# The entry of the in-projection: a written order for VectorE and ScalarE until the second row is there

## The chip, the cores and the metric

The kernel runs on one core of one Trainium2 chip. The metric is the device time of one execution in microseconds (us). The engines are called as the profile calls them: PE (TensorE, matrix products; PEld are its weight loads), DVE (VectorE), ACT (ScalarE), POOL (GpSimd) and SP (SyncE, which issues the transfers from memory here).

## The reference

The reference is one inference step of a two-layer diffusion backbone. Two groups of 128 tokens, a prompt and a sample, go through the same weights; the model width D is 2048. Layer 0 mixes latent attention and grouped-query attention behind one combined in-projection, layer 1 uses differential attention; each layer ends in a gated convolutional feed-forward part. What the change touches is the very beginning of layer 0:

```python
mod = jax.nn.silu(cond) @ w_ada[l] + b_ada[l]
sh1, sc1, gt1, sh2, sc2, gt2 = jnp.split(mod[:, None, :], 6, axis=-1)
h = rmsnorm(x, g_norm_mix[l]) * (1 + sc1) + sh1
...
proj = h @ w_in
```

So the shift `sh1` and the scale `sc1` come out of a product of the condition with two of the six column blocks of `w_ada`; the tokens are normalised, scaled and shifted; and the result `h` is multiplied by `w_in`, a matrix of 2048 rows and 2880 columns. Everything is in float32.

## The kernel before

**Tiling.** Features lie on the 128 partitions, and the 2 x 128 tokens side by side in the free dimension (`NT` = 256). `h` is therefore cut into 16 rows of 128 features, "row k" below, and `w_in` into blocks of 128 x 128: 16 rows by `NIN` = 23 output columns. Every product is made of three matmuls, since a value is held as a high part (rounded to the type that PE multiplies fast) and a low part (the rest): high weight by high row, high weight by low row, low weight by high row. Three such matmuls with one block are called a chain link here, or a chain for short where only one row is at hand.

**Weights.** `Stream` (from L303 on) brings `w_in` in raw tiles of 16 blocks (1 MB; three buffers) with `fetch` on SP. `block` hands out one block after the other; when it has none left it cuts a piece from the raw tile, 4 blocks the first time and 8 later, and `split` (L225) makes the two parts: a cast on ACT (`wh`, L226) and a subtraction on DVE (`wl`, L227). There are four buffers for `wh` and four for `wl`.

**Modulation by units.** `Early` computes shift and scale for one row (the first four units) or for two rows (the other six). `load(1)` and `load(0)` bring the two pieces of `w_ada` (tiles `araw` and `condb`) on SP; `sums` (L412) multiplies them with the condition, with 32 small matmuls for a unit of one row; `turn` (L420) copies the result from the accumulator to `am` on ACT; `finish` transposes `am` on PE (L427) and makes `mod` and `scl` from it by three small instructions on DVE (L430, L433, L435).

**Norm.** The squares of `x` are added up by ACT and DVE, PE takes the mean (L846), `rstd` finishes it with one instruction on DVE (L189) and a power on POOL (L193), `diagonal` writes it on two diagonals (DVE, L213) and `spread` (PE, L221) spreads it over all partitions; that is `rb0`.

**A row.** `modulate` makes row `c`: `x` by `rb0` on DVE (L587), scale and shift for the one half of the tokens on DVE (L595) and for the other on ACT (L598), the high part `hx` by a cast on ACT (L599), the low part by a subtraction (L582) on DVE for even rows and POOL for odd ones.

**Order of the work.** PE runs an order that is written out: each of its instructions in this stage is pinned behind the one before it by `keep_in_program_order`. The order begins with unit 0's first sums, the mean of the norm, unit 0's second sums, the spread, unit 0's transposes and unit 1's first sums. Then `held` runs row 0 through columns 0 to 9 (`HELD` = 10; their accumulators stay in five banks) with unit 1's second sums after column 1 and its transposes after column 4, then row 1 through the same ten columns, and `others` runs rows 0 and 1 through columns 10 to 22 with the sums of units 2 and 3 between them. Then come rows 2 and 3, and from there four rows at a time. The transfers of this stage that are shown as `pin` are pinned on SP in the same manner. On DVE and ACT nothing is pinned in the entry: a planner that steps through the program with its own estimate of every duration and landing puts an instruction where its engine is free and its inputs are taken to be there. So the cast of a later piece of weights can come ahead of a step that the next row waits for. An engine runs its instructions in the planned order and does not pass one that waits.

Of the kernel before, what the change touches and what calls it, by code (L numbers as in the profile page):

```python
# [22 lines left out]
NT = 2 * T  # L23
# [5 lines left out]
EPS = 1e-6  # L29
# [59 lines left out]
def step_kernel(ctx: ExitStack, tc: tile.TileContext, A: dict):  # L89
    nc = tc.nc  # L90
    pe, dve, act, pool, sp = nc.tensor, nc.vector, nc.scalar, nc.gpsimd, nc.sync

    keep = ctx.enter_context(tc.tile_pool(name="keep", bufs=1))
    wpool = ctx.enter_context(tc.tile_pool(name="wpool", bufs=3))
    tmp = ctx.enter_context(tc.tile_pool(name="tmp", bufs=2))
# [37 lines left out]
    x = T_(keep, [P, KD, NT], "x")  # L133

    mod = T_(keep, [P, NL, 6, KD, 2], "mod")
    scl = T_(keep, [P, NL, 2, KD, 2], "scl")
# [9 lines left out]
        tc.keep_in_program_order(sp.dma_start(out=ada["cw"], in_=A["wconv"][:, l]))  # L146


    chains = []

    def step():
# [31 lines left out]
    def rstd(cols, n, factor=1.0, out=None):  # L183

        v = T_(small, [P, 2], "rv")
        at = 0
        for ps in cols:
            w = n // len(cols)
            dve.tensor_scalar(out=v[:, at:at + w], in0=ps, scalar1=EPS, scalar2=factor ** -2,  # L189
                              op0=ALU.add, op1=ALU.mult)  # L190
# [19 lines left out]
    def diagonal(r, cols):  # L210
        dg = T_(tmp, [P, 2 * T], "diag", bufs=1)
        for i, c in enumerate(cols):
            dve.tensor_scalar(out=dg[:, i * T:(i + 1) * T], in0=ident, scalar1=r[:, c:c + 1],  # L213
                              scalar2=None, op0=ALU.mult)
        return dg

    def spread(dg, cols=(0, 1), bank=bank):

        ps = bank()
        n = len(cols) * T  # L220
        pe.matmul(ps[:, :n], ones, dg[:, :n], start=True, stop=True)  # L221
        return ps[:, :n]


    def split(out_hi, out_lo, src, pin=lambda i: i):  # L225
        pin(act.copy(out_hi, src))  # L226
        pin(dve.tensor_tensor(out=out_lo, in0=src, in1=out_hi.bitcast(F32), op=ALU.subtract))  # L227
# [72 lines left out]
    class Stream:  # L300
# [7 lines left out]
        def fetch(self, pin=lambda i: i):  # L308
# [3 lines left out]
            self.raws.append((raw, self.sizes[self.at]))  # L312
            self.at += 1

        def block(self):
            if not self.blocks:
                if not self.raws:
                    self.fetch()
                raw, n = self.raws[0]
                m = min(8, n - self.lo) if self.lo or self.at > 2 else 4  # L320
                wh = T_(wpool, [P, 1024 + P], "wh", F32R, bufs=4)[:, :m * P]
                wl = T_(wpool, [P, 1024 + P], "wl", F32R, bufs=4)[:, :m * P]
                split(wh, wl, raw[:, self.lo * P:(self.lo + m) * P])
                self.blocks = [(wh[:, b * P:(b + 1) * P], wl[:, b * P:(b + 1) * P]) for b in range(m)]
                self.lo += m
                if self.lo == n:
                    self.raws.pop(0)
                    self.lo = 0
            return self.blocks.pop(0)

    def by_token(pieces, xs, outs, first, last):
# [58 lines left out]
    class Early:  # L390
# [26 lines left out]
        def turn(self):  # L417
            n = 2 * self.n
            am = T_(tmp, [P, 512], "am", bufs=1)
            act.copy(am[:, :n * P], self.ps[:, :n * P])  # L420
            self.am = am

        def finish(self):
            n = 2 * self.n
            pt = att_bank()
            for b in range(n):
                tc.keep_in_program_order(pe.transpose(pt[:, b * P:(b + 1) * P], self.am[:, b * P:(b + 1) * P], ident))  # L427
            c = slice(self.c0, self.c0 + self.n)
            out = mod[:, 0, 0:2, c]
            dve.tensor_reduce(out=out, axis=AX.X, op=ALU.add,  # L430
                              in_=pt[:, :n * P].rearrange("p (j c g r) -> p j c r g", j=2, g=4, r=32)[:, :, :, 0:2])
            bada = C("bada").rearrange("p (l j k) -> p l j k", l=NL, j=6)
            dve.tensor_tensor(out=out, in0=out, op=ALU.add,  # L433
                              in1=bada[:, 0, 0:2, c, None].to_broadcast([P, 2, self.n, 2]))
            dve.scalar_tensor_tensor(out=scl[:, 0, 0, c], in0=mod[:, 0, 1, c], scalar=1.0, op0=ALU.add, op1=ALU.mult,  # L435
                                     in1=C("gmix")[:, c, None].to_broadcast([P, self.n, 2]))

    def vector(name, l, j, q):

# [277 lines left out]
    def mixer_ab(hx, W, units, st):  # L717
        l = 0
        with tc.tile_pool(name="ab", bufs=1) as ab:
            with tc.tile_pool(name="abp", bufs=1) as pj:  # L720
# [118 lines left out]
                for to, of in ((squares[0], squares[1]), (squares[0], squares[2]), (squares[0], squares[3]),  # L839
                               (pr[:, 0:2], pr[:, 2:4])):  # L840
                    dve.tensor_tensor(out=to, in0=to, in1=of, op=ALU.add)
                units[0].sums(1)
                ps = bank()
                for g in range(2):
                    for k in range(2):
                        tc.keep_in_program_order(pe.matmul(ps[:, g:g + 1], pr[:, k, g * T:(g + 1) * T], inv(D),  # L846
                                                           start=(k == 0), stop=(k == 1)))
                units[0].sums(0)
                r = rstd([ps[:, 0:2]], 2)
                units[0].turn()  # L850
                units[0].finish()
                rb0 = spread(diagonal(r, (0, 1)))

                def product(ps, c, ks, first, last):
                    pin = (lambda i: i) if free[0] else tc.keep_in_program_order
# [58 lines left out]
                held(banks_, [0], rows, at(c1=[lambda: u1.sums(0), u1.turn, lambda: W.fetch(pin), lambda: load(u3), lambda: W.fetch(pin)],  # L914
                                           c4=[lambda: end(u1)]))
                held(banks_, [1], rows, at())
                others(rows, at(c10=[lambda: u2.sums(1)], c12=[lambda: u2.sums(0), u2.turn], c14=[lambda: end(u2)],
                                c17=[lambda: u3.sums(1)], c20=[lambda: u3.sums(0), u3.turn], c22=[lambda: end(u3)]))
                for q in range(4):
                    banks_ = side()  # L920
                    if q == 0:
                        rows = range(2, 4)
                        held(banks_, [2], rows, at())
                        held(banks_, [3], rows, at())
                    else:
                        u = units[2 * q + 3]
                        rows = range(4 * q, 4 * q + 4)
# [17 lines left out]
            with tc.tile_pool(name="abh", bufs=1) as hp:  # L945
# [36 lines left out]
                for h in range(0, 8, 2):  # L982
                    for i in range(2):
                        ps = gemm(WQ.chunk(), qh, qlo)
# [3 lines left out]
                    ps = gemm(WQ.chunk(), qh, qlo)  # L988
# [7 lines left out]
                    for i in range(2):  # L996
# [3 lines left out]
                        ps = gemm(WK.chunk(), kh, klo, 3 * T)  # L1000
# [219 lines left out]
    with banks("pab") as ppool["ada"]:  # L1220
# [3 lines left out]
        units = [Early(k, 1) for k in range(4)] + [Early(c, 2) for c in range(4, KD, 2)]  # L1224
        W = Stream(A["w_in_ab"], ([TB] * 5 + [12]) * 4)
# [13 lines left out]
    with tc.tile_pool(name="cc", bufs=1) as cp, banks("pc") as ppool["ada"]:  # L1239
        ada["junk"] = lambda: T_(cp, [P, 4, 512], "junk", BF16, bufs=1)  # L1240
        ppool["att"] = ppool["ada"]
        W = Weights(A["w_in_c"], KD, 1)
        hx, ready, todo = modulated(st, 1, 0, W, True)
# [4 lines left out]
        W = Weights(A["w_up"][1], KD, 1)  # L1248
        hx, ready, todo = modulated(st, 1, 1, W, True)
# [153 lines left out]
```

## Time and profile before

| | |
|---|---|
| median of the runs | 2328.17 us |
| lowest and highest of 3 runs | 2324.3 and 2330.32 us |
| the profiled execution | 2326.47 us |
| its span, from the first to the last instruction | 2324.7 us |
| PE busy in the span | 2278.1 us |
| bytes moved | 610.82 MB, 263 GB/s on average |

The rows shown below come from several views. The page counts busy time for each engine. The waits say which engine stood still for whom. A row of the timeline begins with the start and the busy time of an instruction (or of several like ones, "x32"), then engine, line, operation, output <- inputs; a bracket at its end gives the idle time ahead of it and what ended it. A row of the windows gives a stretch, its length, the busy time of PE, PEld, DVE, ACT and POOL with their counts, the granted clock of PE, the share of the DMA engines and the rate of transfer.

### The profile page before, as it was taken

How to read it: one execution, taken by the hardware profiler on the slowest of the kernel's cores; microseconds unless marked ns; L12 is line 12 of the kernel's file. 1: busy time of each engine (PE TensorE's matmuls, PEld its weight loads, DVE VectorE, ACT ScalarE, POOL GpSimd, SP SyncE). 2: the span in 40 equal slices, each digit the busy share in tenths (PEclk: the TensorE clock that was granted, in tenths of full speed). 3: DMA queues.
4: the chain of work that ended last, by engine and by line, in shares of the span. 5: the costliest groups of instructions: out<-in, count | busy, mean ns of one | idle time of the engine just before them, and what ended most of it. 6: DMA issues, size and time to landing. Idle time of an engine off the chain costs nothing. (4 is left out here: it accounts for less than half of the span.)

```text
span 2324.7 us, 47404 instructions
## 1 busy us (share of the span) xinstructions
PE 2278.1 (98%) x19810; PEld 2186.6 (94%) x19810; DVE 1827.7 (79%) x2654; ACT 1178.2 (51%) x1866; POOL 145.6 (6%) x133
## 2 busy tenths in 40 slices
PE   6999999999999999999999999999999999999998
PEld 6888878799999999999989999898999999999998
DVE  4667749789989999999869989787899755666654
ACT  4347554555554355554465555446555434555553
POOL 0002001200000000002210000022000000000011
PEclk9999999999999999999999999999999999999999
DMA  9997789666777777777767787785677555555553
GB/s 388 364 376 254 280 315 386 258 250 252 272 259 285 289 279 257 263 266 278 272 237 274 276 316 297 296 312 222 236 256 272 186 196 200 190 192 200 191 192 125
DMA packets 92566, 610.82 MB, mean 263 GB/s; under 512 B 9984, under 2 KB 17856, under 8 KB 20544
## 3 DMA queue, kind: packets, MB, share of 16 engines
q1 hardware_dynamic: 92352, 607.80, 70.8%
q8 instruction: 155, 2.54, 0.4%
q14 instruction: 59, 0.48, 0.1%
HBM read 603.01 MB, written 4.75 MB: 261 GB/s over the span
## 5 line engine op out<-in xcount | busy, mean ns | idle before, releaser
L226 ACT CAST wh<-raw 128x1024 fp32r<-128x1024 f32 (+1 forms) x789 | 793.7, 1012 | 927.7 <-PE acc L375 694.4
L227 DVE TENSOR_TENSOR wl<-raw,wh 128x1024 fp32r<-128x1024 f32 (+1 forms) x789 | 924.6, 1187 | 315.5 <-ACT wh L226 305.6
L374 PE MATMUL acc<-hx,wh 128*128 128x256 f32 x3440 | 952.6, 277 | 1.3 <-ACT wh L226 0.8
L375 PE MATMUL acc<-hx,wh 128*128 128x256 f32 x3440 | 951.8, 277 | 0.0
L378 PE MATMUL acc<-hx,wl 128*128 128x256 f32 x3440 | 951.6, 277 | 0.1
L374 PEld LDWEIGHTS acc<-hx,wh 128*128 128x128 f32 x3440 | 646.0, 188 | 7.7 <-issue 5.0
L378 PEld LDWEIGHTS acc<-hx,wl 128*128 128x128 f32 x3440 | 645.7, 188 | 5.4 <-issue 3.4
L375 PEld LDWEIGHTS acc<-hx,wh 128*128 128x128 f32 x3440 | 646.1, 188 | 2.7 <-issue 2.5
L484 DVE CUSTOM_DVE_ANT_0 junk<-araw,condb 128x2048 f32<-128x2048 f32 (+1 forms) x192 | 442.8, 2307 | 0.1
L375 PE MATMUL acc<-g,wh 128*128 128x256 f32 x1408 | 388.3, 276 | 0.0
L378 PE MATMUL acc<-g,wl 128*128 128x256 f32 x1408 | 388.0, 276 | 0.0
L374 PE MATMUL acc<-g,wh 128*128 128x256 f32 x1408 | 387.8, 276 | 0.0
L375 PEld LDWEIGHTS acc<-g,wh 128*128 128x128 f32 x1408 | 264.3, 188 | 0.0
L378 PEld LDWEIGHTS acc<-g,wl 128*128 128x128 f32 x1408 | 264.2, 188 | 0.0
L374 PEld LDWEIGHTS acc<-g,wh 128*128 128x128 f32 x1408 | 264.1, 188 | 0.0
L181 POOL TENSOR_TENSOR sqacc<-sqacc,sq 128x256 f32<-128x256 f32 x62 | 85.4, 1377 | 1574.4 <-issue 1298.3
L859 PE MATMUL acc<-hx,wh 128*128 128x256 f32 x608 | 113.7, 287 | 3.9 <-ACT hx L599 3.0
L859 PEld LDWEIGHTS acc<-hx,wh 128*128 128x128 f32 x608 | 93.9, 191 | 12.0 <-issue 4.8
L1172 ACT ACTIVATE cv<-acc,convw 128x256 f32<-128x256 f32 x176 | 98.3, 559 | 2.4 <-PE acc L362 2.4
L648 DVE SCALAR_TENSOR_TENSOR x<-acc,mod,x 128x128 f32<-128x128 f32 x192 | 58.0, 343 | 41.5 <-PE acc L378 40.5
L1178 DVE SCALAR_TENSOR_TENSOR cv<-acc,convw,cv 128x254 f32<-128x254 f32 x176 | 84.3, 479 | 3.7
L1175 DVE SCALAR_TENSOR_TENSOR cv<-acc,convw,cv 128x254 f32<-128x254 f32 x176 | 83.6, 475 | 2.5 <-ACT cv L1172 2.5
(253 smaller groups left out, 2492.4 us busy)
## 6 DMA issues: line engine op xcount, KB each, us to landing
raw<-w_up SPq DMA_DIRECT2D x176, 1024.0 KB, 4.8
araw<-w_ada SPq DMA_DIRECT2D x160, 1024.0 KB, 5.4
raw<-w_down SPq DMA_DIRECT2D x88, 1024.0 KB, 4.8
raw<-w_in_c SPq DMA_DIRECT2D x48, 1024.0 KB, 5.5
raw<-w_in_ab SPq DMA_DIRECT2D x20, 1024.0 KB, 8.4
araw<-w_first SPq DMA_DIRECT2D x16, 1024.0 KB, 8.7
condb<-w_first SPq DMA_DIRECT2D x16, 1024.0 KB, 10.4
raw<-w_out_ab SPq DMA_DIRECT2D x16, 1024.0 KB, 7.4
```

The source lines that it names most:

```text
L181: pool.tensor_tensor(out=st["acc"], in0=st["acc"], in1=sq, op=ALU.add)
L226: pin(act.copy(out_hi, src))
L227: pin(dve.tensor_tensor(out=out_lo, in0=src, in1=out_hi.bitcast(F32), op=ALU.subtract))
L374: fixed(pe.matmul(ps[:, :n], wh, xh(k), start=(i == 0), stop=False))
L375: fixed(pe.matmul(ps[:, :n], wh, xl(k), start=False, stop=False))
L378: fixed(pe.matmul(ps[:, :n], wl, xh(k), start=False, stop=(i == last)))
L484: tc.keep_in_program_order(dve.tensor_tensor_reduce(out=junk, in0=raw, in1=condb[:, c].rearrange("p (g n) -> p g n", g=4), scale=1.0, scal ...
L648: dve.scalar_tensor_tensor(out=x[:, c, s], in0=ps[:, s], scalar=mod[:, l, 3 * which + 2, c, g:g + 1], in1=x[:, c, s], op0=ALU.mult, op1=AL ...
L859: pin(pe.matmul(ps, w, hx[:, k, lo:lo + NT], start=first and k == ks[0] and n == 0, stop=last and k == ks[-1] and n == 2, skip_group_check ...
L1172: pin(act.activation(y, ps, AF.Identity, scale=cw[:, 1, m:m + 1], bias=cw[:, 3, m:m + 1]))
L1175: pin(dve.scalar_tensor_tensor(out=y3[:, :, 1:], in0=p3[:, :, :T - 1], scalar=cw[:, 0, m:m + 1], in1=y3[:, :, 1:], op0=ALU.mult, op1=ALU.add))
L1178: pin(dve.scalar_tensor_tensor(out=y3[:, :, :T - 1], in0=p3[:, :, 1:], scalar=cw[:, 2, m:m + 1], in1=y3[:, :, :T - 1], op0=ALU.mult, op1=A ...
```

## The change

A new helper `tie` pins an instruction behind the one before it on its engine as long as a flag is set. The flag goes up ahead of `rstd` and down when the second row is there. In between, the instructions of `rstd`, `diagonal`, `spread`, `turn` and `finish` are tied, and so are those of two new functions, `start_row` (the multiply by `rb0`) and `finish_row` (scale, shift, high part, low part), which take the place of `modulate` for rows 0 and 1. The low part of row 1 is thereby made on DVE; it was on POOL.

`Stream.piece(m, pin)` cuts a piece of up to `m` blocks when it is called, and is called at written places: 4 blocks ahead of the spread, 8 behind row 0, 4 when unit 1's second sums are issued, 4 behind row 1. Outside of these places `block` cuts pieces of 8 as before, always of 8 where more than 8 are left of a raw tile.

On PE, unit 1's second sums go from behind column 1 to behind column 3 of row 0, and its transposes from behind column 4 to behind column 6. The two fetches and the loads of unit 3, which are issued on SP, move with the sums.

```diff
+    tied = [False]
+
+    def tie(i):
+        return tc.keep_in_program_order(i) if tied[0] else i
...
@@ class Stream
+        def piece(self, m, pin=lambda i: i):
+            if not self.raws:
+                self.fetch()
+            raw, n = self.raws[0]
+            m = min(m, n - self.lo)
+            wh = T_(wpool, [P, 1024 + P], "wh", F32R, bufs=4)[:, :m * P]
+            wl = T_(wpool, [P, 1024 + P], "wl", F32R, bufs=4)[:, :m * P]
+            split(wh, wl, raw[:, self.lo * P:(self.lo + m) * P], pin)
+            self.blocks += [(wh[:, b * P:(b + 1) * P], wl[:, b * P:(b + 1) * P]) for b in range(m)]
...
         def block(self):
             if not self.blocks:
...
-                m = min(8, n - self.lo) if self.lo or self.at > 2 else 4
...
+                self.piece(8)
             return self.blocks.pop(0)
...
@@ mixer_ab
+                def start_row(c):
+                    h = T_(tmp, [P, NT], "nt", bufs=4)
+                    tie(dve.tensor_tensor(out=h, in0=x[:, c], in1=rb0, op=ALU.mult))
+
+                    def finish_row():
+                        a_, b_ = (lambda g: scl[:, 0, 0, c, g:g + 1]), (lambda g: mod[:, 0, 0, c, g:g + 1])
+                        tie(dve.tensor_scalar(out=h[:, :T], in0=h[:, :T], scalar1=a_(0), scalar2=b_(0),
+                                              op0=ALU.mult, op1=ALU.add))
+                        tie(act.activation(h[:, T:], h[:, T:], AF.Identity, scale=a_(1), bias=b_(1)))
+                        tie(act.copy(hx[:, c, :NT], h))
+                        tie(dve.tensor_tensor(out=hx[:, c, NT:2 * NT], in0=h, in1=hx[:, c, :NT].bitcast(F32),
+                                              op=ALU.subtract))
+
+                    return finish_row
+
                 units[0].sums(1)
...
                 units[0].sums(0)
+                tied[0] = True
                 r = rstd([ps[:, 0:2]], 2)
+                dg = diagonal(r, (0, 1))
+                W.piece(4, tie)
+                rb0 = spread(dg)
                 units[0].turn()
+                first_row = start_row(0)
                 units[0].finish()
-                rb0 = spread(diagonal(r, (0, 1)))
+                first_row()
+                W.piece(8, tie)
...
                 u1, u2, u3 = units[1:4]
-                scale(units[0])
                 load(u2)
                 u1.sums(1)
                 rows = range(0, 2)
                 banks_ = side()
-                held(banks_, [0], rows, at(c1=[lambda: u1.sums(0), u1.turn, lambda: W.fetch(pin), lambda: load(u3), lambda: W.fetch(pin)],
-                                           c4=[lambda: end(u1)]))
+                second = []
+
+                def fresh():
+                    W.piece(4, tie)
+                    second.append(start_row(1))
+                    u1.turn()
+
+                def second_row():
+                    u1.finish()
+                    second[0]()
+                    W.piece(4, tie)
+                    tied[0] = False
+
+                held(banks_, [0], rows, at(c3=[lambda: u1.sums(0), fresh, lambda: W.fetch(pin), lambda: load(u3),
+                                               lambda: W.fetch(pin)],
+                                           c6=[second_row]))
                 held(banks_, [1], rows, at())
```

More of the change, by code (lines that the diff above doesn't have):

```diff
@@ L188, in rstd @@
             w = n // len(cols)
-            dve.tensor_scalar(out=v[:, at:at + w], in0=ps, scalar1=EPS, scalar2=factor ** -2,
-                              op0=ALU.add, op1=ALU.mult)
+            tie(dve.tensor_scalar(out=v[:, at:at + w], in0=ps, scalar1=EPS, scalar2=factor ** -2,
+                                  op0=ALU.add, op1=ALU.mult))
             at += w
@@ L212, in diagonal @@
         for i, c in enumerate(cols):
-            dve.tensor_scalar(out=dg[:, i * T:(i + 1) * T], in0=ident, scalar1=r[:, c:c + 1],
-                              scalar2=None, op0=ALU.mult)
+            tie(dve.tensor_scalar(out=dg[:, i * T:(i + 1) * T], in0=ident, scalar1=r[:, c:c + 1],
+                                  scalar2=None, op0=ALU.mult))
         return dg
@@ L220, in spread @@
         n = len(cols) * T
-        pe.matmul(ps[:, :n], ones, dg[:, :n], start=True, stop=True)
+        tie(pe.matmul(ps[:, :n], ones, dg[:, :n], start=True, stop=True))
         return ps[:, :n]
@@ L313, in fetch @@
             self.at += 1
+        def piece(self, m, pin=lambda i: i):
[7 more added lines that the diff above has]
+            self.blocks += [(wh[:, b * P:(b + 1) * P], wl[:, b * P:(b + 1) * P]) for b in range(m)]
+            self.lo += m
+            if self.lo == n:
+                self.raws.pop(0)
+                self.lo = 0
         def block(self):
             if not self.blocks:
-                if not self.raws:
-                    self.fetch()
-                raw, n = self.raws[0]
-                m = min(8, n - self.lo) if self.lo or self.at > 2 else 4
[L321 to L328, printed above, removed]
+                self.piece(8)
             return self.blocks.pop(0)
@@ L419, in turn @@
             am = T_(tmp, [P, 512], "am", bufs=1)
-            act.copy(am[:, :n * P], self.ps[:, :n * P])
+            tie(act.copy(am[:, :n * P], self.ps[:, :n * P]))
             self.am = am
@@ L429, in finish @@
             out = mod[:, 0, 0:2, c]
-            dve.tensor_reduce(out=out, axis=AX.X, op=ALU.add,
-                              in_=pt[:, :n * P].rearrange("p (j c g r) -> p j c r g", j=2, g=4, r=32)[:, :, :, 0:2])
+            tie(dve.tensor_reduce(out=out, axis=AX.X, op=ALU.add,
+                                  in_=pt[:, :n * P].rearrange("p (j c g r) -> p j c r g",
+                                                              j=2, g=4, r=32)[:, :, :, 0:2]))
             bada = C("bada").rearrange("p (l j k) -> p l j k", l=NL, j=6)
[L433 to L436, printed above, removed]
+            tie(dve.tensor_tensor(out=out, in0=out, op=ALU.add,
+                                  in1=bada[:, 0, 0:2, c, None].to_broadcast([P, 2, self.n, 2])))
+            tie(dve.scalar_tensor_tensor(out=scl[:, 0, 0, c], in0=mod[:, 0, 1, c], scalar=1.0,
+                                         op0=ALU.add, op1=ALU.mult,
+                                         in1=C("gmix")[:, c, None].to_broadcast([P, self.n, 2])))
     def vector(name, l, j, q):
```

## The prediction

> **What bounds the kernel now.** I read the page first, then the waits of PE in the first 40 us, then the clock and the transfers by windows, then the timeline of the two places where PE stands still.
>
> ```profile
> span 2324.7 us, 47404 instructions
> PE 2278.1 (98%) x19810; PEld 2186.6 (94%) x19810; DVE 1827.7 (79%) x2654; ACT 1178.2 (51%) x1866; POOL 145.6 (6%) x133
> ```
>
> PE is busy for 98% of the span, so a microsecond that it loses anywhere arrives at the end, and all of its idle time is 2324.7 − 2278.1 = 46.6 us. Its waits from 0 to 24 us, and from 24 to 40 us (total us, times, longest):
>
> ```profile
> PE ada L412 <- DMA araw<-w_first: 12.8, 1, 12.8
> PE acc L859 <- ACT hx L599: 1.4, 1, 1.4
> ...
> PE acc L859 <- ACT hx L599: 1.6, 1, 1.6
> PE acc L859 <- POOL hx L582: 0.4, 1, 0.4
> ```
>
> The first wait, for the first weights to land, is not touched by the change. The other three are: 1.4 us before the product of row 0, 1.6 us before that of row 1, and 0.4 us for the low half of row 1. Each has a second price, the clock. These windows follow the steps in which the granted clock changes (stretch, its length, busy time of PE, PEld, DVE, ACT and POOL with counts, granted clock, DMA share, GB/s):
>
> ```profile
> 19.58:22.99 3.41, 1.50 (x36) 1.06 (x35) 2.69 (x8) 1.37 (x4) 0.00 (x0) 1.00 1.00 418
> 22.99:26.40 3.41, 3.41 (x38) 2.77 (x38) 0.36 (x1) 0.00 (x0) 0.00 (x0) 0.50 1.02 416
> ...
> 29.82:33.23 3.41, 1.38 (x9) 0.98 (x9) 1.37 (x4) 0.90 (x2) 0.73 (x1) 1.00 1.02 423
> 33.23:36.64 3.41, 3.41 (x18) 3.41 (x17) 0.00 (x0) 1.56 (x3) 0.00 (x0) 0.50 1.01 420
> ...
> 1166.45:1169.86 3.41, 2.23 (x16) 1.20 (x16) 1.80 (x5) 0.74 (x3) 0.70 (x1) 1.00 0.80 195
> 1169.86:1173.27 3.41, 3.41 (x14) 1.13 (x12) 2.80 (x7) 2.19 (x5) 0.62 (x1) 0.50 0.97 396
> 1183.51:1186.93 3.42, 2.38 (x18) 1.97 (x18) 2.95 (x5) 3.40 (x7) 0.88 (x2) 1.00 0.16 22
> 1186.93:1190.34 3.41, 3.41 (x32) 3.41 (x31) 3.29 (x5) 1.78 (x4) 2.67 (x3) 1.00 0.97 392
> ```
>
> A window of 3.41 us with PE busy for 1.50, 1.38 or 2.23 us (44, 40 and 65%) is followed by one at clock 0.50; one with 2.38 us (70%) is not. So each stall in the entry costs half of 3.41 us, 1.7 us, on top of itself.
>
> **Row 0.** PE's fixed order here is the second sums of unit 0, the spread of the norm, unit 0's transposes, unit 1's first sums, the product.
>
> ```profile
> 16.50 1.93 PE L412 MATMUL ada<-condb,condw 128*32 128x128 f32 x32
> ...
> 17.70 2.08 ACT L226 CAST wh<-raw 128x512 fp32r<-128x512 f32 x3 [6.40 <-DMA raw<-w_in_ab]
> ...
> 18.36 1.22 PE L221 MATMUL misc<-diag,cst 128*128 128x256 f32 x2
> ...
> 19.69 0.36 ACT L420 COPY am<-ada 128x256 f32<-128x256 f32 x1
> 20.10 0.44 PE L427 MATMUL att<-cst,am 128*128 128x128 f32 x2 [0.52 <-ACT am L420]
> ...
> 20.47 1.08 PE L412 MATMUL ada<-araw,condw 128*32 128x128 f32 x32
> ...
> 21.37 0.17 DVE L430 TENSOR_REDUCE mod<-att 128x4 f32<-128x16 f32 x1
> ...
> 22.95 1.04 PE L859 MATMUL acc<-hx,wh 128*128 128x256 f32 x2 [1.40 <-ACT hx L599]
> 23.40 0.29 PEld L859 LDWEIGHTS acc<-hx,wh 128*128 128x128 f32 x1 [0.18 <-DVE hx L582]
> ```
>
> The sums end at 16.50 + 1.93 = 18.43, but ACT casts three pieces of weights (4, 8 and 4 blocks) from 17.70 and copies `am` only at 19.69. Tied, it casts one piece of 4 (about a quarter of 2.08 and some start, 0.6) and copies at about 18.5. The transposes then wait only for the spread, to 18.36 + 1.22 = 19.58, and end 0.44 later at 20.02. DVE has the multiply of row 0 behind it and reduces at about 20.07 in place of 21.37: **1.30 us** sooner. From the reduction to the product nothing changes (22.95 − 21.37 = 1.58), so the product starts at 21.65. Unit 1's first sums, 1.08 us, still fit between. In the window to 22.99 PE would be busy for 0.44 + 1.08 + 1.1 = 2.6 us, 77%, above the 70% that kept the clock.
>
> **Row 1.** The same kinds of step, now in the order that the planner chose:
>
> ```profile
> 24.77 1.85 PE L412 MATMUL ada<-condb,condw 128*32 128x128 f32 x32
> ...
> 26.72 1.05 ACT L226 CAST wh<-raw 128x1024 fp32r<-128x1024 f32 x1 [3.82 <-DMA raw<-w_in_ab]
> ...
> 27.68 0.36 ACT L420 COPY am<-ada 128x256 f32<-128x256 f32 x1
> ...
> 28.09 0.44 PE L427 MATMUL att<-cst,am 128*128 128x128 f32 x2 [0.23 <-ACT am L420]
> ...
> 28.73 0.39 PE L859 MATMUL att<-hx,wh 128*128 128x256 f32 x2
> ...
> 28.94 0.17 DVE L430 TENSOR_REDUCE mod<-att 128x4 f32<-128x16 f32 x1
> ...
> 29.41 0.39 PE L859 MATMUL att<-hx,wh 128*128 128x256 f32 x2
> ...
> 30.43 0.41 DVE L587 TENSOR_TENSOR nt<-x,misc 128x256 f32<-128x256 f32 x1
> ...
> 31.86 0.38 PE L859 MATMUL acc<-hx,wh 128*128 128x256 f32 x1 [1.61 <-ACT hx L599]
> ...
> 32.67 0.38 PE L859 MATMUL acc<-hx,wh 128*128 128x256 f32 x1 [0.42 <-POOL hx L582]
> ```
>
> A cast stands ahead of `am`, and subtractions and the multiply of row 1 (30.43) stand between the reduction (28.94) and the product (31.86): 2.92 us, where row 0 took 1.58. A chain of three matmuls is (29.41 − 28.73) / 2 = 0.34 us at full clock. By the new order, step by step: chain 0 starts at 21.65 and waits for its low half as now (23.40 − 22.95 = 0.45), so four chains end at 21.65 + 0.45 + 0.23 + 3 × 0.34 = 23.35. Unit 1's second sums, at the 1.08 of the row at 20.47 and no longer at 1.85, end at 24.43. ACT copies `am` to 24.85 while PE does chains 4 to 6, to 25.5. Transposes to 25.95, reduction at 26.0, plus 1.58: **row 1 starts at 27.58 in place of 31.86, 4.28 us sooner** (the 1.30 included). Chains 7 to 9 fill PE to 27.0, so about 0.6 us of stall stay. The low half moves from POOL to DVE: 32.67 − 31.86 = 0.81 becomes row 0's 0.45, **0.36 us**. With 0.6 + 0.35 us idle in a window PE is busy for 72%, just over the 70% row: the window at half clock goes, **1.7 us**, with the bounds 0 and 1.7 since the margin is thin. Entry together: 4.28 + 0.36 + 1.7 = **6.3 us** (4.6 without the clock).
>
> Edits that I cost at nothing: the next raw tile is cut 4 + 8 + 4 in place of 8 + 8, and the casts above price that: 2.08 for 4 + 8 + 4 against twice 1.05. The piece of 4 and its subtraction, tied ahead of the second `am` and the multiply of row 1, end near 24.6, while PE is in chains 4 to 6; with that cover gone they would cost the 0.6 of a cast. SP's order stays: the third fetch, unit 3's loads and the fourth fetch move with the second sums, which end earlier than now. Behind the tied `am` copy ACT holds row 1's activation and cast, which need it anyway.
>
> **What is late next: the transfers.** The memory queue is full from the start:
>
> ```profile
> 40.00:48.00 8.00, 8.00 (x114) 7.34 (x114) 2.75 (x8) 5.17 (x12) 0.00 (x0) 1.00 1.01 416
> 48.00:54.00 6.00, 6.00 (x76) 5.67 (x75) 4.36 (x11) 4.44 (x10) 0.00 (x0) 1.00 0.89 300
> ...
> 58.00:64.00 6.00, 5.94 (x65) 5.10 (x67) 5.60 (x11) 1.68 (x2) 0.00 (x0) 1.00 0.79 283
> 64.00:78.00 14.00, 13.80 (x164) 10.33 (x160) 10.04 (x21) 5.19 (x8) 0.75 (x1) 1.00 1.00 404
> ```
>
> ```profile
> 67.99 1.19 SPq L403 DMA_DIRECT2D condb<-w_first  x2
> ...
> condb<-w_first SPq DMA_DIRECT2D x2, 1024.0 KB, 7.4
> ...
> 77.56 1.07 PE L412 MATMUL ada<-condb,condw 128*32 128x256 f32 x16 [0.20 <-DMA condb<-w_first]
> ```
>
> It moves some 420 GB/s up to 48 us and has room only in 48 to 54 (300) and 58 to 64 (283): (120 + 137) × 6 / 420 = 3.7 us of transfer; by the DMA shares, (0.11 + 0.21) × 6 = 1.9 us. At 77.56 PE already waits 0.2 us for unit 5's last tile, with no room before it. If PE asks 6.3 us sooner, the idle stretches fill up, and this tile can land 3.7 us sooner and no more (bounds 1.9 and 4.2, the latter with the 404 GB/s of 64 to 78, 16 × 14 / 420 = 0.5 us more). **So 6.3 − 3.7 = 2.6 us come back as one wait at that place.** A stall of 2.6 us lies in one or two windows and should halve the next one (1.7 us); if the first gain is only 4.6, the stall is 0.9 us and does not. I take half of 1.7, 0.85.
>
> The Trainium skill's page "TensorE: Matmul & The Clock Gate", section "HAM oscillation — how this bites in real kernels", gives as rule that PE gaps under about 3.4 us do not bring the clock down. This trace disagrees, since 1.4 and 1.6 us did; by the rule the 0.85 above would be 0.
>
> **Sum.** −6.3 + 2.6 + 0.85 = −2.85 us. Against the profiled execution, 2326.47 us (span 2324.7 and 1.8 around it), that is 2323.6. The median of the runs shown is 2328.17, 1.7 above it, so on that scale 2328.17 − 2.85 = **2325.3 us**. From this cause alone: −1.9 + 1.7 = −0.2 to −6.3, and with the 3 us by which the shown runs stand off their median, 2320.5 to 2330.
>
> **Rivals.** (1) *The transfers do not cap it.* Requests shift in order, other tiles give way, and the whole 6.3 us stays: 2321.9. For it: PE waits only 0.2 us on a transfer after the start. Against it: that wait is at a tile behind a queue with 1.00 share. (2) *The stall at 77.56 does not bring the clock down*, since stalls under a full window do not, in which case the two half-clock windows of the entry have another cause and stay: 3.7 us are left, 2324.5. That is the rule of "TensorE: Matmul & The Clock Gate" in the Trainium skill; for it, one window at 70% kept its clock; against it, three at 65% and less did not. (3) *The order is not as tight as written.* Only listed steps are tied; the next 8-block cast of the second raw tile is not. The planner now puts such a cast ahead of `am`, where it waits for a landing at 26.72. Then `am` comes at 27.7 as before, the reduction at 28.7 (transposes behind it), the product 1.58 later at 30.3: 31.86 − 30.3 + 0.36 = 1.9 us gained, the half clock stays, the transfers do not bind: 2326.3. (4) *Slower: the clock's grid.* Everything after the entry moves by some microseconds against the 3.41 us windows, and gaps that today fall astride two windows fall into one. A place is 1183.51, at 70%, a hair above the 65% that halves. Each such window costs 1.7 us; from two on the 2.85 us are gone, and three make 2328.17 − 2.85 + 5.1 = 2330.4. Against it, the same shift can free windows that are halved today, like the one after 1166.45.
>
> **How the numbers follow.** Forecast 0.40, rival 1 0.17, rival 2 0.14, rival 3 0.14, rival 4 0.15. The range 2320 to 2331 leaves out the lower third of rival 1 (0.06), the upper third of rival 4 (0.05) and the tails of the rest (0.09). About what a measurement of this kernel can tell from no change is 0.3%, 7 us: faster means under 2321.2, slower over 2335.2. Under 2321.2 lie 0.4 of rival 1 (0.07) and the low ends of the others (0.05): 0.12. Over 2335.2 lies only a grid that goes wrong four times and more, 0.05. The rest, 0.83, is within.
>
> **What would show it.** Right: row 0's product near 21.65 and row 1's near 27.6, the cast of 8 blocks behind row 0's hx on ACT, DVE in place of POOL for row 1's low half, no window at 0.50 between 23 and 37 us; then PE waiting 1 to 3 us for `condb` in the sums of unit 5, near 72 to 74 us, and the 48 to 64 us stretches at over 400 GB/s. Wrong: no wait for a transfer there while later stages begin 5 us or more sooner (rival 1); a cast waiting for raw ahead of the second `am` (rival 3); a stall of over 1.2 us in a window without a halved one behind it (rival 2); an entry that gains as written while the end does not, with more windows at 0.50 than now (rival 4).

## The result and the profile after

The changed kernel takes 2323.46 us (median of 20 runs, 2319.56 to 2328.19) where the kernel before, timed beside it, takes 2329.74 us (20 runs, 2323.62 to 2333.61). The ratio is **0.9977, with the interval 0.9969 to 0.9984**: 5.4 us faster, between 3.7 and 7.2. The forecast was 2.85 us faster and 2325.3 us. The profiled execution has a span of 2319.3 us.

The waits of PE in the first 24 us, from 24 to 40 and from 40 to 82 us, in the profile after:

```profile
PE ada L420 <- DMA araw<-w_first: 13.3, 2, 13.0
...
PE acc L890 <- ACT hx L861: 0.6, 1, 0.6
PE acc L890 <- ACT proj L896: 0.2, 1, 0.2
...
PE ada L420 <- DMA condb<-w_first: 1.3, 1, 1.3
PE acc L890 <- POOL hx L592: 0.4, 1, 0.4
PE ada L420 <- DMA araw<-w_first: 0.4, 1, 0.4
```

The 1.4 us ahead of row 0 are gone, of the 1.6 us ahead of row 1 0.6 are left. The wait of 0.4 us for an `araw` tile is new, and the one for unit 5's last `condb` tile has grown from 0.2 to 1.3 us. The timeline after, at the two rows:

```profile
17.90 0.62 ACT L231 CAST wh<-raw 128x512 fp32r<-128x512 f32 x1 [6.42 <-DMA raw<-w_in_ab]
...
18.70 0.37 ACT L428 COPY am<-ada 128x256 f32<-128x256 f32 x1 [0.18 <-PE ada L420]
...
20.24 0.17 DVE L438 TENSOR_REDUCE mod<-att 128x4 f32<-128x16 f32 x1
...
21.83 0.84 PE L890 MATMUL acc<-hx,wh 128*128 128x256 f32 x2
...
23.75 1.08 PE L420 MATMUL ada<-condb,condw 128*32 128x128 f32 x32
...
24.90 0.37 ACT L428 COPY am<-ada 128x256 f32<-128x256 f32 x1 [1.66 <-PE ada L420]
...
26.35 0.17 DVE L438 TENSOR_REDUCE mod<-att 128x4 f32<-128x16 f32 x1 [1.43 <-PE att L435]
...
27.91 0.42 DVE L862 TENSOR_TENSOR hx<-nt,hx 128x256 fp32r<-128x256 f32 x1 [0.61 <-ACT hx L861]
27.94 0.84 PE L890 MATMUL acc<-hx,wh 128*128 128x256 f32 x2 [0.58 <-ACT hx L861]
```

ACT copies `am` right behind the first piece, row 0's product starts at 21.83 (22.95 before), and row 1's at 27.94 (31.86), each 1.6 us behind its reduction. Windows of the same trace (busy times of PE, PEld, DVE, ACT, POOL, granted clock, DMA share, GB/s), first in the entry, then over the transfers that the prediction spoke of, then around the last wait:

```profile
19.58:22.99 3.41, 3.00 (x42) 2.16 (x41) 1.92 (x7) 2.11 (x4) 0.00 (x0) 1.00 1.02 423
22.99:26.40 3.41, 3.41 (x54) 3.09 (x53) 1.98 (x4) 0.63 (x2) 0.00 (x0) 1.00 1.01 413
26.40:29.82 3.42, 2.76 (x22) 2.37 (x21) 2.34 (x7) 2.83 (x6) 0.00 (x0) 1.00 1.02 422
...
48.00:54.00 6.00, 5.55 (x49) 5.35 (x49) 5.33 (x10) 2.65 (x5) 1.16 (x1) 1.00 1.02 419
...
58.00:64.00 6.00, 6.00 (x77) 4.35 (x70) 3.53 (x5) 2.68 (x3) 0.00 (x0) 1.00 1.01 419
...
72.18:75.60 3.42, 2.08 (x28) 1.41 (x25) 0.64 (x1) 0.59 (x1) 0.00 (x0) 1.00 1.01 422
75.60:79.01 3.41, 3.41 (x32) 3.41 (x31) 1.74 (x6) 1.71 (x3) 0.00 (x0) 1.00 1.01 420
```

No window of the entry is at 0.50. The two stretches that moved 300 and 283 GB/s before move 419 now. And the window with PE busy for 2.08 of 3.42 us, 61%, is not followed by half clock. The wait in it, with the end of unit 5's work:

```profile
71.20 1.07 PE L420 MATMUL ada<-condb,condw 128*32 128x256 f32 x16
73.61 1.07 PE L420 MATMUL ada<-condb,condw 128*32 128x256 f32 x16 [1.34 <-DMA condb<-w_first]
76.08 0.60 PE L435 MATMUL att<-cst,am 128*128 128x128 f32 x4
```

Since PE does the same products in the same order in both programs from column 10 of rows 0 and 1 on, its n-th weight load in one trace can be set against the n-th in the other. The table gives these shifts against the first trace of the kernel before (us; minus is sooner), for it and the kernels below, each from one execution; the heads are times of the first trace. The column for row 1 is taken at its low half, 32.67 us in the first trace; row 1's product itself starts 3.92 us sooner in the changed kernel (31.86 to 27.94). The last column is the timed ratio. One run of the last but one kernel, of 6773.5 us, was slow and is left out of its ratio.

```
                     row 1  col 10 unit 4  unit 5     at     at     at     at   ratio [interval]
                     32.67   37.69  62.67   80.0    160    230   1000   2300
changed              -4.27   -5.90  -5.65  -3.97  -3.97  -3.94  -4.70  -5.36   0.9977 [0.9969, 0.9984]
changed, again       -4.44   -5.95  -5.76  -4.14  -4.14  +0.10  -0.70  -1.64
before, again        -0.12   -1.73  -1.73  -1.50  -1.48  +2.60  +3.81  +1.61
ninth tile late      -4.59   -6.22  -5.95  -5.30  -5.09  -0.79  -2.37  -2.85   0.9982 [0.9973, 0.9990]
two tiles late       -4.31   -5.82  -5.62  -4.37  -4.37  -4.35  -4.26  -5.58   0.9973 [0.9961, 0.9985]
PE's places before   -5.14   -6.65  -4.13  -3.70  -3.70  -3.69  -5.91  -6.07   0.9976 [0.9965, 0.9988]
untied               -1.56   -3.18  -3.20  -1.78  -1.78  -1.66  -3.78  -3.98   0.9990 [0.9979, 1.0000]
row 1 tied           -0.57   -2.19  -2.02  -1.41  -1.41  -1.41  -3.65  -3.99   0.9991 [0.9976, 1.0006]
row 0 tied           -0.02   -1.63  -1.63  -0.79  -0.79  +4.18  +1.96  +1.62   1.0002 [0.9992, 1.0013]
changed, tile out    -4.50   -6.01  -5.80  -5.72  -5.72  -5.72 -11.28 -12.38   0.9958 [0.9944, 0.9973]
before, tile out     -0.49   -0.46  -0.44  -0.85  -0.85  -0.01  -5.60  -3.27   0.9955 [0.9940, 0.9970]
```

The first line holds most of the story: 5.9 us won by column 10, 1.9 us of them given back (1.7 at unit 5, the rest ahead of unit 4), 4.0 us carried out of the stage, and then a drift to 5.4 that needs an explanation of its own. From about 70 us on the instructions of the two programs are the same and in the same order on PE, DVE, ACT and POOL (the last difference is an instruction of DVE at 70.2 us in the trace after), so the drift is no work that the change added or removed.

### The profile page after: what moved, and what is told of

It is laid out like the page before. It is cut to its first block, busy times and chain, and to the rows that moved or that the text cites. A ratio compares the mean times of both kernels' runs of the same rounds, so it can differ in the third digit from the quotient of the medians.

```text
span 2319.3 us, 47408 instructions
## 1 busy us (share of the span) xinstructions
PE 2274.0 (98%) x19810; PEld 2183.1 (94%) x19810; DVE 1828.3 (79%) x2656; ACT 1177.4 (51%) x1867; POOL 145.8 (6%) x132
```

## The experiments

Theory: the written order wins by taking casts and subtractions from ahead of the two rows' steps, and the memory queue returns part of it at unit 5's last tile. Rivals: the parts that look important are not (the ties, or PE's new places), or what is given back comes from elsewhere.

### Without the ties

```diff
-                tied[0] = True
```

> The changed kernel with the flag never raised: pieces at their written places, rows 0 and 1 by the new functions, PE's new places, but DVE and ACT free for the planner. Theory: the ties carry the gain. ACT casts three pieces ahead of the first copy again (row 0 at 22.9 in place of 21.83) and two pieces of the second raw tile, which lands at 26.7, ahead of the second copy (row 1 at 30 to 31 us in place of 27.94); windows at half clock come back; columns 10 on start at most 1.5 us ahead of the kernel before. Rival: the written places and PE's order are enough: row 1 within 0.5 us of 27.94.

ACT's and DVE's rows ahead of row 1, in this kernel's timeline:

```profile
26.32 1.57 ACT L231 CAST wh<-raw 128x512 fp32r<-128x512 f32 x2 [3.08 <-DMA raw<-w_in_ab]
...
27.80 0.36 ACT L428 COPY am<-ada 128x256 f32<-128x256 f32 x1
...
29.07 0.17 DVE L438 TENSOR_REDUCE mod<-att 128x4 f32<-128x16 f32 x1
```

Row 0 is not sooner (+0.35 us), row 1 starts at 30.6 us, columns 10 on 3.2 us sooner and the stage ends 1.8 us sooner. The planner puts two casts of the second raw tile ahead of the `am` copy, whose sums had ended at 26.3; they wait for a landing at 26.3 and the copy comes at 27.80. The theory holds for the rows: the ties carry 2.7 of the 3.9 us at row 1's product, and more than half of what leaves the stage (2.2 of 4.0 us). The time, 0.9990, agrees. One point of the expectation failed: no window at half clock came back, and columns 10 on gained 3.2 us instead of at most 1.5.

### Row 0 alone, row 1 alone

For row 0 alone the flag goes down behind row 0, and unit 1 is as before:

```diff
                 W.piece(8, tie)
+                tied[0] = False
...
-                held(banks_, [0], rows, at(c3=[lambda: u1.sums(0), fresh, ...], c6=[second_row]))
+                held(banks_, [0], rows, at(c1=[lambda: u1.sums(0), u1.turn, ...], c4=[lambda: end(u1)]))
```

For row 1 alone it goes up at that place:

```diff
-                tied[0] = True
                 r = rstd([ps[:, 0:2]], 2)
...
                 W.piece(8, tie)
+                tied[0] = True
```

> Only row 0 of the change: ties and written pieces until row 0 is there, then unit 1 as before (second sums after column 1, transposes after column 4, planner's order, low half of row 1 on POOL). Theory one: the parts add. Row 0 starts 1.1 us sooner, the window from 23 us is not at half clock (1.7 us), and columns 10 on start 2.8 us sooner than before. Theory two: the cast ahead of unit 1's copy waits for the landing of the second raw tile at 26.7 us, whatever PE does; row 1 then starts at 31.9 us as before, PE only stands longer ahead of it (3 to 4 us), the next window is at half clock, and columns 10 on start within 0.3 us of the kernel before: row 0's part by itself is worth nothing.

> The changed kernel with the flag raised only behind row 0: DVE and ACT are free for the planner up to there, so row 0 starts as before, near 22.9 to 23 us, and the window at half clock from about 23 us comes back. Unit 1 and row 1 are tied as in the change. If the transfers of unit 5 set what can be kept, row 0's part (1.1 us and 1.7 us of clock) is nearly worthless at the end of the stage: columns 10 on start some 3.3 to 3.7 us ahead of the kernel before, PE waits under 0.7 us for unit 5's tiles, and the stage leaves 3.3 to 3.7 us ahead, next to the 3.97 of the whole change. If the parts simply add and nothing caps them, what is missing at column 10 (2.8 us of 5.9) is missing at the end of the stage too, in the same share: 2.0 us ahead or less.

Row 0 alone, from its timeline and its windows:

```profile
21.14 0.41 ACT L861 CAST hx<-nt 128x256 fp32r<-128x256 f32 x1
...
26.70 1.04 ACT L231 CAST wh<-raw 128x1024 fp32r<-128x1024 f32 x1 [3.68 <-DMA raw<-w_in_ab]
27.65 0.36 ACT L428 COPY am<-ada 128x256 f32<-128x256 f32 x1
...
24.47:27.89 3.42, 0.71 (x7) 0.51 (x5) 0.11 (x1) 1.19 (x2) 0.00 (x0) 1.00 1.01 414
27.89:31.30 3.41, 3.23 (x15) 3.23 (x16) 3.24 (x7) 1.52 (x3) 0.00 (x0) 0.50 1.00 418
```

Row 0 comes 1.3 us sooner, and row 1 at 31.84, as in the kernel before: unit 1's sums end at 23.9 already, but the cast ahead of `am` waits until 26.70 for its landing. PE stands for 2.9 us and the next window is at 0.50. So for row 1 theory two is right: **row 0's gain is lost at the next landing that the planner has put in the way**. Columns 10 on still start 1.6 us sooner, where theory two said at most 0.3: the kernel before had half clock from 33.2 to 36.6 in its first trace, under row 1's chains, this one from 27.9 to 31.3, under row 0's last chains, behind which PE would have waited for row 1's `hx` in any case (its cast ends at 31.8 us in this trace). The time, 1.0002, shows no gain.

Row 1 alone misses its numbers: columns 10 on 2.2 us sooner, not 3.3 to 3.7, and out of the stage 1.4 us, in the same share as in the whole change (64 and 67%). In this execution the clock was low from the start until about 28 us (unit 1's second sums, 1.08 us after the change, took 1.94), so `am` came only at 28.47. A cap at a fixed time does not fit this. A fixed share does not fit all the kernels either: of what they had won by column 10, row 0 alone keeps 48% at the end of the stage, the untied kernel 56%, and the second execution of the kernel before 86% of its 1.73 us. Neither part alone is told from no change by the timed runs (0.9991 and 1.0002), and both together are.

### PE's places as before

```diff
-                held(banks_, [0], rows, at(c3=[lambda: u1.sums(0), fresh, ...], c6=[second_row]))
+                held(banks_, [0], rows, at(c1=[lambda: u1.sums(0), fresh, ...], c4=[second_row]))
```

> The changed kernel with PE's places as they were before: unit 1's second sums behind column 1, its transposes behind column 4; the ties and pieces stay. By my reading of the changed kernel's timeline row 1 then starts some 0.6 to 0.9 us sooner than its 27.94, at 27.1 to 27.4, and the stall of 0.58 us ahead of it goes, since the transposes come sooner and five chains of row 0 cover the rest. The in-projection still leaves at 3.97 us, since unit 5's last tile sets that: the wait for it grows by what the entry gains. Rival: the move on PE carries part of the gain, and row 1 starts later than 27.94, at 28.5 or more, since copy and transposes then meet DVE's subtractions.

Row 1 starts at 27.06 us, 0.9 us sooner than in the changed kernel, without the stall of 0.58 us, and columns 10 on 0.75 us sooner: the move on PE carries none of the gain. The stage leaves 3.70 us ahead, as expected, but not for the reason given. Of its lead 2.5 us go already before unit 4. Here the planner put a subtraction between the steps of a later row, whose product waited 1.4 us (the waits of PE from 26 to 56 us), and at 57.6 us PE waited another 0.6 us for a sum on DVE (`proj`, L898):

```profile
PE acc L890 <- ACT hx L609: 1.4, 1, 1.4
PE acc L890 <- POOL hx L592: 0.4, 1, 0.4
```

The wait for unit 5's last tile is then 0.7 us. The time, 0.9976, is that of the change.

### The raw tiles behind unit 5's

The ninth raw tile (`at == 8`) goes behind unit 5's four tiles on SP; in a second kernel the tenth also goes behind unit 6's first two:

```diff
             if not self.raws:
-                self.fetch()
+                if self.at == 8:
+                    with tc.issue_after(units[5].last.ins):
+                        self.fetch()
+                else:
+                    self.fetch()
...
-                pin(sp.dma_start(out=raw, in_=A["w_first"][self.c0 + t, j]))
+                self.last = pin(sp.dma_start(out=raw, in_=A["w_first"][self.c0 + t, j]))
```

> The changed kernel with one more order on SP: the ninth raw tile of the in-projection is issued behind unit 5's four tiles and no longer ahead of them. If the memory queue gives back part of the entry's gain (PE waited 0.39 us and 1.34 us for unit 5's tiles in the changed kernel), these tiles come one transfer of 1 MB, some 2.5 us, sooner; both waits go, the second half of unit 5's second sums starts near 71.9 in place of 73.61 us, and the in-projection leaves 5.6 to 5.7 us ahead of the kernel before in place of 3.97. If what was given back has another cause (the planner's order after the entry, the clock), the waits or the end stay as they are, at 3.97. The end: 1.7 us below the changed kernel by the first, equal by the second.

> The changed kernel with the ninth raw tile issued behind unit 5's tiles, and the tenth behind the first two of unit 6's. In the kernel with the ninth alone, unit 5's last tile still shared the memory queue with both raw tiles, issued at 63.3 and 64 us, and PE waited 0.76 us for it. With the tenth away the wait should fall to 0.3 us or less and the stage leave 5.6 to 6 us ahead of the kernel before. If instead the tile's own issue (PE frees its buffer at 62.9 us) sets its landing, the wait stays at 0.7 us. The end: 1.3 to 2 us below the changed kernel, which single executions cannot tell.

With the ninth tile late, the 0.39 us wait is gone and the other one is 0.76 us, and the stage leaves 5.1 to 5.3 us ahead: 1.1 to 1.3 us more than the changed kernel, where 1.7 were expected, and 0.3 us of it was there at unit 4 already. With two tiles late the wait is 1.3 us again, against both of the numbers I gave, so that one trace alone speaks for the order on SP. From the kernel with two tiles late: the transfers issued at 59.05 us (unit 5's second `araw` tile) and at 63.23 us (its last `condb` tile) with their us to landing, and the window between the two landings:

```profile
araw<-w_first SPq DMA_DIRECT2D x1, 1024.0 KB, 7.3
...
condb<-w_first SPq DMA_DIRECT2D x1, 1024.0 KB, 9.9
...
66.30:73.12 6.82, 5.56 (x69) 3.67 (x67) 5.66 (x11) 3.17 (x6) 1.17 (x1) 1.00 1.01 419
```

The `araw` tile landed at 66.3 us, the `condb` tile at 73.1. In between 6.82 × 419 GB/s = 2.86 MB went by, though in the order of issue only the two `condb` tiles of 1.05 MB lay there. So part of a tile that was issued later passed ahead, and a place in the order of issue is only part of the remedy. The times, 0.9982 and 0.9973, are those of the change within their intervals: no version that beats it can be named.

### Without unit 5's last tile

```diff
             for t in range(self.n):
+                if j == 0 and t == 1 and self.c0 == 6:
+                    self.raws[j].append(self.raws[j][0])
+                    continue
```

> The changed kernel without the transfer of unit 5's last tile (its sums use the tile before it twice; the scale and shift of one row are therefore not the reference's). In the changed kernel PE waited 1.3 to 1.4 us for this tile. If that tile is where the entry's gain is given back, the wait goes and the stage leaves 5.2 to 5.6 us ahead of the kernel before, next to the 5.65 of the stretch ahead of unit 5's sums. If the give-back belongs to the memory queue as a whole, the next tile of the queue takes the wait over: PE waits 1 us or more for another tile of units 5 to 7 and the stage leaves 4.5 us ahead or less.

> The kernel before without the transfer of unit 5's last tile (its sums use the tile before it twice). PE waited 0.2 to 0.4 us for it. By the first reading of the pair the stage gains 0.2 to 0.4 us against the same execution's shift ahead of unit 5's sums, so that without this tile the two kernels lie 5 us and more apart at the end of the stage, if both leave the cold clock at the same time, and 3.5 us if not. By the second the wait moves to another tile, of the same length.

PE's waits from 36 to 165 us in the changed kernel without the tile:

```profile
PE acc L893 <- POOL hx L595: 0.3, 1, 0.3
PE ada L423 <- DMA araw<-w_first: 0.2, 1, 0.2
```

The wait is gone, no other tile takes it over, and the stage leaves 5.72 us ahead where unit 4 had 5.80. The traffic around it is the same: a tile of unit 6 is issued in its place at 63.05 us and lands at 73.42 us, where the tile left out was issued at 63.20 and landed at 73.56 us in the changed kernel. So it is PE's need of that tile that went, not the load on the queue. In the kernel before the same cut is worth 0.4 us. **That one tile is where the entry's gain is given back**; at the end of the stage the pair lies 4.87 us apart (5.72 − 0.85) where the two kernels with the tile lay 3.97.

The rest of these two runs must be kept apart. Both gain 5.6 us more between 230 and 1000 us: with one transfer less the planner made another order for the next stage (PE's order differs from 180 us on), in which the stall for `diag` at the entry of the first feed-forward part is 0.6 us in place of 1.9 and the one of 2.0 us or more for `hx` is gone; but PE waits 1.1 us (changed) and 2.6 us (before) for a tile of `w_ada` in their place, so what makes up the 5.6 us is not shown in full. For the times, this hides the pair's difference: 0.9958 and 0.9955, with intervals of 3.5 us to each side, do not show the 4.87 us, and do not exclude them.

### Both kernels once more

> The changed kernel once more, for another execution's trace. If what lies between 3.97 us at the end of the stage and 5.4 us at the end of the profiled execution comes from the windows at half clock later on, which fall differently in each execution, the stage leaves 3.8 to 4.2 us ahead again, and the shift at the end is another, by 1 to 5 us, with its jumps at the windows at half clock. If it belongs to the change, the shift at the end is 5.4 again within 0.4 us.

> The kernel before once more. By the same reasoning its trace up to the end of the in-projection's entry repeats within 0.4 us, with half clock behind both stalls, and the later windows at half clock (265, 436, 1170, 1583 us in the first execution) come in another number or length, each worth 1.7 us for 3.4 us. If they belong to the program they come at the same places with the same lengths.

The changed kernel repeats itself up to 160 us (3.97 and 4.14 us ahead). At 2300 us it is 1.6 us ahead and not 5.4. The windows at the place where 4.2 us of that went, first in this trace, then in the first one of the changed kernel, each cut where its own trace's clock steps lie:

```profile
205.85:209.26 3.41, 2.72 (x21) 1.72 (x21) 3.12 (x15) 2.15 (x5) 1.48 (x2) 1.00 0.97 387
209.26:219.50 10.24, 10.24 (x39) 8.02 (x40) 5.50 (x21) 8.14 (x19) 2.17 (x3) 0.50 0.65 237
```

```profile
205.30:208.71 3.41, 2.66 (x21) 1.56 (x19) 2.99 (x13) 1.95 (x5) 1.18 (x2) 1.00 0.98 384
208.71:218.95 10.24, 9.82 (x73) 7.45 (x70) 6.49 (x23) 8.65 (x21) 2.47 (x4) 1.00 0.74 273
```

The same work, nearly the same share of PE in the window ahead (80 and 78%), and 10.24 us at half clock in the one execution and none in the other. So what comes behind 160 us differs between executions of one program by as much as the change is worth. The first trace's drift from 3.97 to 5.36 is smaller than that; which windows make it up is not shown.

The kernel before does not repeat its entry. Its sums, the window of the second stall and the one behind it, in the second trace:

```profile
20.78 1.94 PE L412 MATMUL ada<-araw,condw 128*32 128x128 f32 x32
24.83 1.94 PE L412 MATMUL ada<-condb,condw 128*32 128x128 f32 x32
...
30.68:34.10 3.42, 1.94 (x14) 1.74 (x15) 0.39 (x2) 1.49 (x3) 0.73 (x1) 1.00 1.01 422
34.10:37.51 3.41, 3.41 (x52) 3.28 (x55) 1.14 (x2) 3.30 (x5) 0.00 (x0) 1.00 1.01 420
```

Sums that took 1.08 us at 20.47 in the first trace take 1.94, so the clock was still low at 22.7; and the stall of row 1, 1.5 us here and 1.6 in the first trace, is not followed by half clock. Here the window's edges lie elsewhere against the stall, so that PE is busy for 57% of the window and not for 40%. Columns 10 on come 1.7 us sooner for that. The expectation that the entry repeats is refuted. It is not the rule either: the kernel before without unit 5's last tile, whose entry is the same, has half clock behind both stalls again (its windows around the second one):

```profile
30.14:33.55 3.41, 1.76 (x12) 1.56 (x13) 0.56 (x2) 1.37 (x3) 0.73 (x1) 1.00 1.02 423
33.55:36.96 3.41, 3.41 (x18) 3.41 (x17) 0.28 (x1) 2.54 (x5) 0.00 (x0) 0.50 1.01 420
```

So two of three executions of the old entry pay for the second stall in clock. None of the six with both rows tied has half clock there.

## Why the prediction was right, and where it was not

- **The bound: right.** PE's stalls in the entry were the price, and the end moved with them.
- **Row 0, 1.30 us: right.** The reduction came at 20.24 (20.07 forecast), the product at 21.83 (21.65), 1.12 us sooner in a trace that began 0.2 us later.
- **Row 1, 4.28 us, and its low half, 0.36 us: right, a little too large.** The product starts at 27.94 in place of 27.58, 3.92 us sooner, and its low half brings 0.35 us more; 0.6 us of stall are left as forecast, DVE is in place of POOL. The untied kernel shows that the ties do it, the one with row 0 alone that a landing is what stood in the way.
- **The clock, 1.7 us, with 70% as the line: the step that failed.** In the first pair of traces the sum came out: 5.9 us at column 10, 6.3 forecast, 1.6 us of it between row 1's low half and column 10, where the kernel before was at half clock. But the line is not one. Half clock followed a window with 74% (the ninth tile late, at 207.67 us) and 80%, and not one with 61%, nor the second stall of the kernel before in its second execution, with 57%. Against that execution the entry gained 4.2 us (5.95 − 1.73) at column 10, near the 4.6 that the prediction gave as its lower bound. What decides the clock stays open.
- **The transfers, 2.6 us back at unit 5's last tile: right in place and kind, too large.** The sums on it start 3.95 us sooner (77.56 to 73.61; 3.7 forecast), PE waited 1.3 us there and 0.4 at a tile ahead, where 2.6 were forecast. Leaving the tile out removed the wait. As a cap at a fixed time, though, the step is wrong: kernels that gain 1.6 to 3.2 us in the entry gave back 0.8 to 1.4 us too (the second execution of the kernel before, 1.7 us ahead, only 0.2), since the tile is issued when PE has freed its buffer, and its landing takes 8.7 to 10.4 us from there in the ten traces that have it.
- **Half clock behind that wait, 0.85 us: wrong**, there was none, in a window with PE busy for 61%.
- **The sum, 2.85 us: too small.** In the first pair 0.4 us less was gained than forecast, 0.7 us less given back and 0.85 us less lost to the clock, which makes 4.0. Two traces of each kernel put the end of the stage 2.5 to 4.1 us apart, 3.3 us in the mean; the timed runs say 3.7 to 7.2, so the forecast lies below their interval, and that 2323.46 us came out near the 2325.3 forecast is in part luck, as the kernel before was timed 1.6 us above the median that the forecast started from. Every kernel's timed ratio agrees with its shift at the end of the stage against the first trace within its interval (the two without the tile aside). That the timed 5.4 us lie above the traces' mean is left open: no work behind unit 5 differs, and executions differ there by more than that.
- **Rivals.** The uncapped gain of 6.3 us lies inside the timed interval, but the traces show the wait that it denied. Rival 2 has its sign, a stall of 1.3 us without a halved window behind it, but not its price, since the entry's halved windows went. The order was as tight as written. No shift of the later stages against the clock's windows made the kernel slower on the whole, though single executions lost 4 us in that way.

The first sums show when PE leaves the low clock it starts with: before 20.5, during the sums at 20.51 (1.29 us), and past 26.8 us, in three executions. The Trainium skill's page "TensorE: Matmul & The Clock Gate", in the section on Part 1, the clock gate, says that the window of 3413 ns runs free and does not start with the kernel, so that the point of warm-up varies from run to run. These traces agree: all steps of the clock lie 3.41 us or whole multiples of it apart, and the first comes elsewhere in each execution. From before 20.5 to past 26.8 us is more than one such window, though, so where the window lies cannot be the whole reason. Its rule on gaps fares no better than mine: stalls of 1.4 to 2.9 us were followed by half clock here, one of 1.5 us was not.

## What to carry to other kernels

Where a planner orders an engine by its own guess of landings, one large cast in front of a small copy makes the whole chain wait for a transfer that this chain doesn't need; writing down the few steps ahead of the first products is enough to undo it, and only if it is done up to the last of these rows. Before counting such a gain to the end, look for the next transfer whose issue hangs on PE: here a third of the gain went into one tile. And when a change is worth 0.2%, compare the traces at a point behind the change, since single executions differ by as much further on.

## What the runs showed of the hardware that was not expected

- The share of PE's busy time in a window does not decide the clock: 61% kept it (72.18 to 75.60 us after the change), 80% was followed by 10.24 us at half clock, and 78% at the same place in another execution was not. One such stretch costs 4 us, as much as the change is worth, and four of the twelve traces have it near 210 us.
- At the start of the trace the view of windows gives a granted clock of 1.00 while 32 equal small matmuls take 1.93 or 1.94 us, against 1.08 later; the length of equal work shows the low clock where the column doesn't.
- A tile issued later can take part of the transfer ahead of one issued before it: 2.86 MB went by between two landings where two tiles, 2.1 MB, were ahead.
